# A transformer block with 32 experts on one Trainium2 core: the expert stage's bias, token weights and scatter rebuilt, a tenth weight slot, and a shorter front

## The chip, the cores and the metric

The kernel runs on one core of a Trainium2 chip, in one launch. What is measured is the device time of an execution in microseconds (us). Three runs of the kernel before took 1227.55, 1227.74 and 1229.18 us, so the median is 1227.74 us. One more execution was taken by the hardware profiler. It took 1228.12 us in all, and its trace spans 1226.4 us from the first instruction to the last.

The engines are called as in the profile: PE (TensorE, matmuls), PEld (its weight load), DVE (VectorE), ACT (ScalarE), POOL (GpSimd) and SP (SyncE, which here issues nearly all DMAs). PSUM is the memory that PE writes; SBUF is the large on-chip memory; HBM holds the inputs.

## The reference

One layer works on 256 tokens of width 1024, all in float32:

```
mod = silu(c) @ w_ada + b_ada                      # six rows of 1024
h   = rms_norm(x) * (1 + scale1) + shift1
z   = h @ w_in                                     # 1024 -> 7440
ys  = moba(z), gla(z), retention(z), sliding_window(z)   # four mixers of width 256
mixed = sum_n sigmoid(logits_n) * (ys_n @ w_branch[n])   # 1024 merge logits a branch, part of z
x   = x + gate1 * (mixed @ w_out)
h2  = rms_norm(x) * (1 + scale2) + shift2
weights = softmax(top4(h2 @ w_router + b_router))
for e in 32 experts:
    gu  = h2 @ w_gate_up[e] + b_gate_up[e]         # 1024 -> 2048
    act = min(glu,7) * sigmoid(1.702*min(glu,7)) * (clip(lin,-7,7) + 1)
    y  += combine[:, e] * (act @ w_down[e] + b_down[e])   # 1024 -> 1024
x   = x + gate2 * y
out = rms_norm(x) * g_final
```

Every token takes 4 of the 32 experts. All expert weights are read all the same: 8 MB of `w_gate_up` and 4 MB of `w_down` for each expert, 384 MB in all.

## The kernel before, in words

**The front** (to about 300 us). The six `mod` rows are made by DVE (`ada`: rows of `w_ada` times the activation, added up in `acs`; `ada_end` turns the 128 partial sums of a column into one by 8 transposes on PE and two DVE reductions). The input projection is done in blocks of 256 columns (`z_unit`). Each block of weights is split in two float32r parts, `wh` by ACT and `wl` by DVE (`split`, L340 and L341), and PE multiplies hi by hi, hi by lo and lo by hi (`z_part`, L354). The four mixers run as generators between these blocks. Then for each of the four branches the merge gates (`pz_m`), the up-projection (`pu`, L804) and the out projection (`pw`, L758) follow. `gate_rows` (L289) spreads a `mod` row over all partitions by 8 matmuls. The GLA gate (`pga`, L590) takes 24 matmuls, three for each of 8 chunks of channels. In the two softmax mixers each head's values are two matmuls into 64 partitions (L484, L485).

**Memory for weights.** Weights come into slots of 2 MB (128 partitions of 16 KB), or into halves of them in the front. A slot is a buffer of one of several pools: five in `ring`, three in `rx` (opened when the mixers' memory is given up), one in `r9` (opened when the front's memory is given up), nine in all. Another one, `sp`, is used once for `wg0_3`. `slot` hands them out in turn. A load waits on the SP queue until the last reader of its slot is done, and since SP issues in order, all loads behind it wait too. The order is written in the code:

```
units = [wg_src(0, j) for j in range(3)] + [wg_src(1, j) for j in range(4)]
units += [wd_src(0, j) for j in range(2)]
```

`wgE_J` is the J-th quarter of expert E's `w_gate_up`, `wdE_J` half of its `w_down`. The code reaches far ahead by itself: SP runs on as long as there is a free slot.

**The experts** go in quads (`b`, four experts) and pairs (`r`). An expert has 64 places (`CAP`) for its tokens. For a quad, `gather` makes one-hot matrices `pm` on DVE and multiplies the split activations `n2h`, `n2l` with them (`pg`, L998), which gives `he`. `gate_up_bias` (L1056) puts the bias into the two accumulators `ea` and `eb` by matmuls with a column of the identity, in float32. `gate_up_part` (L1065) adds the products, two column groups at a time. `swiglu` (L1038 to L1045) works on DVE and ACT, `act_t` (L1079) transposes its result, `down` (L1092) multiplies by `w_down`, and its result is multiplied by `gate2` on DVE (`oa`, `ob`). POOL multiplies the one-hots by the tokens' weights (`pc`, L1022), PE transposes these (`psm`, L1030), and `scatter` (L1102, float32) adds a pair's result to `x_sb`. The bias of `w_down` is added in four pieces between experts 8 and 15 (`pyb`, L968). `last_pair` treats experts 30 and 31 in pieces, so that the final norm can follow closely.

PE's order in all this is the program's order, with a few instructions placed by `issue_after`.

## Time and profile before

| | |
|---|---|
| median of three runs | 1227.74 us |
| profiled execution, in all | 1228.12 us |
| its span in the trace | 1226.4 us |
| PE busy | 1154.7 us, 94% |
| DVE, ACT, POOL busy | 452.1, 177.0 and 37.0 us |
| read from HBM | 467.81 MB, 382 GB/s over the span |
| the front, first to last instruction before the first expert matmul | 0 to 299.5 us |
| last weight bytes | about 1207 us |

Busy time of PE is not the same as PE being the limit: matmuls are pipelined and their ends are modelled. Read a stage by two questions: are the DMA engines saturated, and what do the engines wait for. An instruction's place in the code is its line, as L354.

### The profile page before, as it was taken

The page shows a single profiled execution, that of the slowest core. Times are in us where ns is not written, and L with a number is a line of the kernel's source. Part 1 is how long each engine was busy: PE and PEld are TensorE (multiplying, and loading weights), DVE is VectorE, ACT ScalarE, POOL GpSimd, SP SyncE. Part 2 cuts the span into 40 slices and gives each one's busy share as a digit, 9 for nine tenths or more (in the row PEclk, how much of TensorE's full clock was granted, in tenths as well). Part 3 has the DMA queues.
Part 4 walks back from the last instruction along what each step waited for, and adds up shares of the span by engine and source line. Part 5 has one row for each costly group of instructions (what it writes and reads, how often), then busy time and mean ns, then how long its engine had stood idle before and what let it go on. Part 6 is the DMA issues. An engine that isn't in the chain of part 4 may idle for free.

```text
span 1226.4 us, 14472 instructions
## 1 busy us (share of the span) xinstructions
PE 1154.7 (94%) x6204; PEld 563.6 (46%) x6204; DVE 452.1 (37%) x764; ACT 177.0 (14%) x293; POOL 37.0 (3%) x105
## 2 busy tenths in 40 slices
PE   6999999999999999999999999999989998999885
PEld 4788899996334333333333333333323332332234
DVE  4577698656222212223132232222221312131213
ACT  3456244444100000000000010000000000000001
POOL 2000000001010000000000000000000000000000
PEclk9999999999999999999999999999999999999998
DMA  9966569848899999999999999999999999999994
GB/s 329 340 267 222 191 236 395 344 187 335 362 429 428 428 428 427 425 428 429 428 428 428 426 428 428 427 427 426 430 428 428 428 428 428 427 428 428 428 421 150
DMA packets 63655, 469.85 MB, mean 383 GB/s; under 512 B 6361, under 2 KB 18754, under 8 KB 39266
## 3 DMA queue, kind: packets, MB, share of 16 engines
q1 hardware_dynamic: 62770, 467.38, 92.4%
q10 hardware_dynamic: 816, 1.49, 0.3%
q8 instruction: 50, 0.82, 0.3%
q14 instruction: 19, 0.16, 0.0%
HBM read 467.81 MB, written 1.05 MB: 382 GB/s over the span
## 4 chain that ended last, share of the span: by engine, by line
PE 70%; DMA 19%; DVE 7%; ACT 1%; issue 1%; POOL 0%; ACTq 0%; SPq 0%; POOLq 0%; DVEq 0%
PE ed L1092 14%; PE ea L1065 13%; PE eb L1065 13%; DMA wd<-in_w_down_dram 12%; DMA wg<-in_w_gate_up_dram 6%; PE pz_m L354 6%; PE py L1102 4%; PE pw L758 2%; PE pg L998 2%; PE pu L804 2%; PE eat L1079 1%; DVE el L1043 1%; DVE el L1045 1%; DVE es L1044 1%; PE psm L1030 1%
## 5 line engine op out<-in xcount | busy, mean ns | idle before, releaser
L1065 PE MATMUL ea<-wg,he 128*64 128x512 f32 x1024 | 279.9, 600 | 6.0 <-DMA wg<-in_w_gate_up_dram 5.6
L1065 PE MATMUL eb<-wg,he 128*64 128x512 f32 x1024 | 278.0, 594 | 0.0
L1092 PE MATMUL ed<-wd,aT 128*64 128x512 f32 x960 | 211.5, 595 | 7.9 <-DMA wd<-in_w_down_dram 6.7
L1039 DVE TENSOR_SCALAR eg<-ea 128x512 f32<-128x512 f32 x32 | 22.1, 692 | 352.5 <-PE ea L1065 349.1
L1065 PEld LDWEIGHTS eb<-wg,he 128*64 128x64 f32 x1024 | 78.4, 137 | 147.8 <-issue 147.7
L1041 ACT ACTIVATE es<-eg 128x512 f32<-128x512 f32 x32 | 20.2, 630 | 816.4 <-DVE eg L1039 816.4
L1065 PEld LDWEIGHTS ea<-wg,he 128*64 128x64 f32 x1024 | 72.1, 137 | 142.5 <-issue 122.9
L1092 PEld LDWEIGHTS ed<-wd,aT 128*64 128x64 f32 x960 | 67.4, 137 | 140.9 <-issue 127.1
L354 PE MATMUL pz_m<-hh,wh_m 128*128 128x256 f32 x256 | 73.1, 286 | 0.0
L354 PE MATMUL pz_m<-hh,wl_m 128*128 128x256 f32 x256 | 72.3, 282 | 0.9 <-DVE wl_m L341 0.9
L354 PE MATMUL pz_m<-hl,wh_m 128*128 128x256 f32 x256 | 71.8, 280 | 0.0
L1102 PE MATMUL py<-oa,sm 128*128 128x512 f32 x60 | 33.7, 643 | 19.5 <-DVE oa L1096 19.4
L1104 DVE TENSOR_TENSOR x_sb<-x_sb,py 128x512 f32<-128x512 f32 x60 | 41.2, 687 | 28.8 <-PE py L1102 28.7
L354 PEld LDWEIGHTS pz_m<-hh,wl_m 128*128 128x128 f32 x256 | 48.2, 188 | 1.3 <-DVE wl_m L341 1.3
L354 PEld LDWEIGHTS pz_m<-hh,wh_m 128*128 128x128 f32 x256 | 48.4, 189 | 0.7 <-ACT wh_b L340 0.3
L354 PEld LDWEIGHTS pz_m<-hl,wh_m 128*128 128x128 f32 x256 | 48.3, 189 | 0.1
L1095 DVE TENSOR_TENSOR oa<-ed,late 64x512 f32<-64x512 f32 x15 | 10.2, 683 | 94.6 <-PE ed L1092 94.6
L1022 POOL TENSOR_TENSOR pc<-pm,comb 128x128 f32<-128x128 f32 x64 | 23.9, 411 | 675.0 <-PE psm L1030 664.4
L1095 DVE TENSOR_TENSOR ob<-ed,late 64x512 f32<-64x512 f32 x15 | 10.2, 683 | 90.0 <-PE ed L1092 90.0
L1056 PE MATMUL ea<-bgu,ident 32*64 32x512 f32 x128 | 36.5, 612 | 0.0
L1056 PE MATMUL eb<-bgu,ident 32*64 32x512 f32 x128 | 36.5, 612 | 0.0
L1079 PEld LDWEIGHTS eat<-ident,el 128*128 128x128 f32 x128 | 17.8, 207 | 37.8 <-DVE el L1045 35.6
(443 smaller groups left out, 1398.4 us busy)
## 6 DMA issues: line engine op xcount, KB each, us to landing
wg<-in_w_gate_up_dram SPq DMA_DIRECT2D x128, 2048.0 KB, 27.7
wd<-in_w_down_dram SPq DMA_DIRECT2D x62, 2048.0 KB, 26.9
wada<-in_w_ada_dram SPq DMA_DIRECT2D x13, 1024.0 KB, 10.7
win_m<-in_w_in_dram SPq DMA_DIRECT2D x11, 1024.0 KB
win_c<-in_w_in_dram SPq DMA_DIRECT2D x8, 1024.0 KB, 16.5
wada<-in_w_ada_dram SPq DMA_DIRECT2D x12, 512.0 KB, 7.2
wada<-in_w_in_dram SPq DMA_DIRECT2D x4, 1024.0 KB, 7.5
win_m<-in_w_ada_dram SPq DMA_DIRECT2D x3, 1024.0 KB
```

What stands on the lines that cost most here:

```text
L354: T.matmul(pz[:, b * 256:(b + 1) * 256], l, r, start=(kh == 0 and b == 0 and kk == 0 and i == 0), stop=last and i == 2, skip_group_check=True)
L758: T.matmul(pw[t, hf_], m_[:, kk, t * P:(t + 1) * P], w[:, 0, :], start=(k == 0 and i == 0), stop=(k == KC - 1 and i == 2))
L804: T.matmul(pu[:, b * S:(b + 1) * S], w[:, k, b * P:(b + 1) * P], yx[:, k, :], start=(i == 0), stop=(i == 5), skip_group_check=True)
L998: last_i["pg"] = T.matmul(pg[:, kk * 256:(kk + 1) * 256], chan(n2[:, t, :], k), pm[:, t].rearrange("p e s -> p (e s)"), start=(i == 0), st ...
L1022: G.tensor_tensor(pc[:, t, :, var, i ^ var, :], pv_[:, :, i, :], cv[:, :, i].unsqueeze(2).to_broadcast([P, EB // 2, CAP]), ALU.mult)
L1039: V.tensor_scalar(g, pa, 7.0, None, ALU.min)
L1056: T.matmul(pp_[64 * j:64 * j + 64, :], ident[r:r + NE, r + e:r + e + 1].to_broadcast([NE, CAP]), bgu[r:r + NE, :], start=True, stop=False, ...
L1065: T.matmul(pp_[64 * j:64 * j + 64, :], he[:, k, (e % EB) * CAP:(e % EB + 1) * CAP], w[:, i * DE + j * 512:i * DE + (j + 1) * 512], start=F ...
L1079: T.transpose(pt[:, q * P:(q + 1) * P], cols, ident)
L1092: T.matmul(pd[64 * jj:64 * jj + 64, :], aT[:, k % 4, 64 * (k // 4):64 * (k // 4) + 64], w[k % 4][:, o * 512:(o + 1) * 512], start=(k == 0) ...
L1102: T.matmul(py, s_[:, hf_, t * P:(t + 1) * P], o, start=True, stop=True)
L1104: V.tensor_tensor(yv, yv, py, ALU.add)
```

## The change

All of it is in one kernel program; the sizes of the experts' weights and the order of the experts are the same.

1. **Bias.** `b_gate_up` is loaded three times, in three blocks of 32 partitions. POOL makes three bf16 parts of it that add up to the float32 value (seven instructions of 2048 elements a partition). A matmul in bf16 with 96 rows of `sel` (three stacked identities) puts the sum into the accumulators. `b_down` lies in the other 32 partitions.
2. **Token weights.** `slot_weights` brings the weights to the experts' 64 places (8 small matmuls and 3 reductions a quad), and `swiglu` multiplies by them. The products `pc` on POOL go; `spread` transposes the one-hots themselves.
3. **Scatter.** The result of `down` is split in hi and lo (ACT copy, DVE subtraction); the scatter is 8 float32r matmuls and runs inside the next pair's `gate_up`. The sums stand in `y_sb`, and `gate2` and `x` come in once, in `x_most`, before the last pair. All of `down_bias` is done at expert 4.
4. **Slots.** `hh` and `hl`, the split activations of the front, lie in one 2 MB buffer of pool `hp`, which becomes a tenth slot when they are no longer read. The one-off `sp` goes. The load order becomes `wg0_0` to `wg0_3`, `wg1_0` to `wg1_3`, `wd0_0`, `wd0_1`. `n2h` and `n2l` live only for the first quad; later gathers split `x_sb` again, a quarter at a time (`n2_split`). In `x_most` the tenth slot is taken for `gate2`, `g_final` and the sums.
5. **Front.** `gate1` is made by two matmuls of a broadcast one with `acs` (which sums the partitions and spreads the sum) and a row of `b_ada` that is loaded to all partitions (512 KB, on ACT's queue), in place of 8 transposes, 2 reductions, `gate_rows(2)` and 2 copies. The GLA gate's hi and lo columns are packed, 16 matmuls in place of 24. Values of the softmax mixers are multiplied for two heads at a time, in two column groups.

The core of the diff:

```diff
+        if s_ == 2:                                    # in ada_end
+                T.matmul(pb, ones[:, 0:1].to_broadcast([P, P]), acc[:, cs], start=True, stop=True)
+                V.tensor_tensor(gate1[:, cs], pb, gate1[:, cs], ALU.add)
...
-            for w, hx in ((wgah, hh), (wgah, hl), (wgal, hh)):
-                T.matmul(pg[0:16, 0:S], w[:, k, :], hx[:, k, :], start=(n == 0), stop=(n == 3 * KC - 1))
+            T.matmul(pg[0:32, 0:S], wgc[:, k, :], hh[:, k, :], start=(k == 0), stop=(k == KC - 1))
+            T.matmul(pg[0:16, 0:S], wgah[:, k, :], hl[:, k, :], start=False, stop=(k == KC - 1), skip_group_check=True)
...
-            if i > 0:
-                values(order[i - 1])
+            if i in (2, 4):
+                values(order[i - 2], order[i - 1])
...
+    A.dma_start(gate1, b_ada[0:1, 2 * D:3 * D].to_broadcast([P, D]))
...
+            for g in range(3):
+                A.dma_start(bt[NE * g:NE * g + NE, :], b_gate_up[0])
+            A.dma_start(bdn, b_down[0])
+            G.tensor_copy(bgu[0:3 * NE, :], bt[0:3 * NE, :])
+            for g0 in (1, 2):
+                for g in range(g0, 3):
+                    r = slice(NE * g, NE * g + NE)
+                    G.tensor_tensor(bt[r, :], bt[r, :], bgu[r, :], ALU.subtract)
+                    G.tensor_copy(bgu[r, :], bt[r, :])
...
+    units = [wg_src(e, j) for e in range(2) for j in range(4)] + [wd_src(0, j) for j in range(2)]
     for u in units[:RING + EXTRA]:
         pref[u[0]] = load_wide(*u)
+    add_slots(hp, 1)
+    for u in units[RING + EXTRA:-1]:
+        pref[u[0]] = load_wide(*u)
...
+        V.scalar_tensor_tensor(sg, sg, w, g, ALU.mult, ALU.mult)          # in swiglu, w: the places' weights
...
+        for jj in range(2):                                               # at the end of down
+            r = slice(64 * jj, 64 * jj + 64)
+            oh, ol = o[jj ^ sw]
+            A.activation(oh[r], pd[r], AF.Copy)
+            V.tensor_tensor(ol[r], pd[r], f32(oh[r]), ALU.subtract)
...
+                gate_up(e, he, range(2))                                  # a pair's start
+                with tc.issue_after(last_i["gu"]):
+                    scatter(*after)
+                gate_up(e, he, range(2, KC))
...
+    def x_most():
+        late = hp.tile([P, 4096], F32, tag="w", name="late")
+        seq.remove(hp)
+        A.dma_start(gfin[0:1, :], g_final.rearrange("(o d) -> o d", o=1))
+        V.tensor_tensor(y_sb, y_sb, gate2.unsqueeze(1).to_broadcast([P, NT, D]), ALU.mult)
+        V.tensor_tensor(xf, x_sb, y_sb, ALU.add)
```

On SP's queue, the loads of the first experts before the change, from the first on (the number at a name's end is that of its buffer):

```order
L134 DMA wg0_0_3154<-in_w_gate_up_dram 128x4096
L134 DMA wg0_1_3156<-in_w_gate_up_dram 128x4096
L134 DMA wg0_2_3158<-in_w_gate_up_dram 128x4096
L134 DMA wg1_0_3160<-in_w_gate_up_dram 128x4096
L134 DMA wg1_1_3162<-in_w_gate_up_dram 128x4096
L134 DMA wg1_2_3164<-in_w_gate_up_dram 128x4096
L134 DMA wg1_3_3166<-in_w_gate_up_dram 128x4096
L134 DMA wd0_0_3168<-in_w_down_dram 128x4096
L134 DMA wg0_3_3310<-in_w_gate_up_dram 128x4096
L134 DMA wd0_1_3312<-in_w_down_dram 128x4096
L134 DMA wd1_0_3522<-in_w_down_dram 128x4096
```

And after it, at the same place of SP's queue:

```order
L134 DMA wg0_0_3133<-in_w_gate_up_dram 128x4096
L134 DMA wg0_1_3135<-in_w_gate_up_dram 128x4096
L134 DMA wg0_2_3137<-in_w_gate_up_dram 128x4096
L134 DMA wg0_3_3139<-in_w_gate_up_dram 128x4096
L134 DMA wg1_0_3141<-in_w_gate_up_dram 128x4096
L134 DMA wg1_1_3143<-in_w_gate_up_dram 128x4096
L134 DMA wg1_2_3145<-in_w_gate_up_dram 128x4096
L134 DMA wg1_3_3147<-in_w_gate_up_dram 128x4096
L134 DMA wd0_0_3149<-in_w_down_dram 128x4096
L134 DMA wd0_1_3242<-in_w_down_dram 128x4096
L134 DMA wd1_0_3524<-in_w_down_dram 128x4096
```

`wg0_3` has moved up from ninth to fourth place and now sits in a slot that is used again. In both, ten loads stand ahead of `wd1_0`, the first that needs a slot which an expert's matmuls have to give back.

On PE, before the change, around the first expert's first quarters (`pg0_2` and `pg0_3` are the gather's third and fourth part; of the gather's matmuls before these rows 22 have run):

```order
L998 MATMUL pg0_2_3369<-pm0_3320,n2h_3138 128x256
L998 MATMUL pg0_2_3369<-pm0_3320,n2l_3251 128x256
L1065 MATMUL ea0_3314<-wg0_0_3154,he0_3330 64x512 x2
L1065 MATMUL eb0_3315<-wg0_0_3154,he0_3330 64x512 x2
L1065 MATMUL ea0_3314<-wg0_0_3154,he0_3330 64x512 x2
L1065 MATMUL eb0_3315<-wg0_0_3154,he0_3330 64x512 x2
L1065 MATMUL ea0_3314<-wg0_1_3156,he0_3330 64x512 x2
```

After it, at the same place:

```order
L1019 MATMUL pg0_3_3372<-pm0_3302,n2h_3250 128x256
L1019 MATMUL pg0_3_3372<-pm0_3302,n2l_3251 128x256
L1124 MATMUL ea0_3296<-wg0_0_3133,he0_3307 64x512 x2
L1124 MATMUL eb0_3297<-wg0_0_3133,he0_3307 64x512 x2
L1124 MATMUL ea0_3296<-wg0_0_3133,he0_3307 64x512 x2
L1124 MATMUL eb0_3297<-wg0_0_3133,he0_3307 64x512 x2
L1124 MATMUL ea0_3296<-wg0_1_3135,he0_3307 64x512 x2
```

30 of the first gather's 32 matmuls now stand ahead of the first expert's, where 24 stood.

On POOL, before the change, from the second mixer's norm to the first pair (`hrsret` is a small power, `ssq2` the router's norm, `pc0` the first quad's weighted one-hots):

```order
L518 TENSOR_TENSOR hrsret_1715<-hvarret_1712,mhalf_86 128x8
L902 TENSOR_TENSOR ssq2_3142<-ssq2_3142,mhalf_86 128x1 x2
L1022 TENSOR_TENSOR pc0_3605<-pm0_3320,comb_3298 128x2x64 x8
```

After it, at the same place:

```order
L528 TENSOR_TENSOR hrsret_1697<-hvarret_1694,mhalf_86 128x8
L794 CAST bias_sb_2303<-bgu32_2305 96x2048
L798 TENSOR_TENSOR bgu32_2305<-bgu32_2305,bias_sb_2303 32x2048 x2
L799 CAST bias_sb_2303<-bgu32_2305 32x2048 x2
L798 TENSOR_TENSOR bgu32_2305<-bgu32_2305,bias_sb_2303 32x2048
L799 CAST bias_sb_2303<-bgu32_2305 32x2048
L935 TENSOR_TENSOR ssq2_3120<-ssq2_3120,mhalf_86 128x1 x2
L1010 CAST pm0_3302<-pm0_3302 128x2x64 x2
```

Seven long instructions for the bias now stand between the mixers and the router; of the one-hots POOL copies two blocks a quad in place of eight products.

## Rows read from the trace of the kernel before

**Rows 1.** Stretches of the span: busy time of each engine, clock, DMA share, GB/s.
```profile
core 0: us, PE busy (x) PEld busy (x) DVE busy (x) ACT busy (x) POOL busy (x), PEclk, DMA share, GB/s
...
30.00:60.00 30.00, 28.46 (x240) 23.59 (x239) 16.87 (x37) 12.13 (x18) 0.00 (x0) 1.00 1.00 340
60.00:150.00 90.00, 89.26 (x673) 76.42 (x673) 67.53 (x132) 44.70 (x91) 2.56 (x1) 1.00 0.61 226
...
300.00:305.00 5.00, 5.00 (x26) 1.70 (x24) 2.54 (x10) 2.03 (x4) 1.78 (x5) 1.00 0.82 279
305.00:310.00 5.00, 5.00 (x28) 2.23 (x26) 0.54 (x1) 0.56 (x1) 1.13 (x4) 1.00 0.90 370
...
315.00:320.00 5.00, 5.00 (x27) 1.37 (x24) 2.67 (x4) 0.63 (x1) 0.00 (x0) 1.00 0.92 392
320.00:325.00 5.00, 5.00 (x24) 1.80 (x23) 0.69 (x1) 0.00 (x0) 0.00 (x0) 1.00 0.34 75
...
330.00:1195.00 865.00, 819.91 (x3690) 286.38 (x3688) 220.24 (x341) 35.34 (x59) 21.04 (x56) 1.00 1.01 427
1195.00:1207.00 12.00, 10.91 (x92) 7.01 (x89) 3.16 (x8) 0.00 (x0) 0.00 (x0) 1.00 0.86 305
1207.00:1227.00 20.00, 7.43 (x84) 6.00 (x82) 8.80 (x21) 3.08 (x8) 1.08 (x1) 0.81 0.17 61
```

**Rows 2.** What SP's queue waited for: us in total, times, longest us.
```profile
SPq L134 <- PE eb L1065: 406.9, 106, 13.5
```

**Rows 3.** Timeline of SP's queue: start us, us, the load issued.
```profile
303.19 0.33 SPq L134 DMA_DIRECT2D wd<-in_w_down_dram  x1
...
306.62 0.33 SPq L134 DMA_DIRECT2D wd<-in_w_down_dram  x1
...
311.36 0.33 SPq L134 DMA_DIRECT2D wg<-in_w_gate_up_dram  x1
...
322.64 0.33 SPq L134 DMA_DIRECT2D wg<-in_w_gate_up_dram  x1
```

**Rows 4.** What PE waited for from 60 to 300: us, times, longest.
```profile
PE pz_m L354 <- DVE wl_m L341: 0.9, 2, 0.7
```

**Rows 5.** The chain that ended last, in order: start us, us, instructions.
```profile
103.28 2.78 PE pga L590 x24
...
391.83 13.88 PE ed L1092 x64
...
408.57 3.82 PE py L1102 x8
```

**Rows 6.** Groups of PE, 60 to 300: count, busy us, mean ns, idle before.
```profile
L260 PE MATMUL pmt<-ident,acs 128*128 128x128 f32 x32 | 5.1, 286 | 0.0
...
L289 PE MATMUL pb<-ident,modT 128*128 128x128 f32 x32 | 4.1, 277 | 0.0
...
L484 PE MATMUL po<-pT,svt 128*64 128x256 f32 x8 | 2.6, 405 | 0.0
...
L485 PE MATMUL po<-pT,svt 128*64 128x128 f32 x8 | 1.6, 279 | 0.0
```

**Rows 7.** One stretch of the front, columns as in rows 1.
```profile
180.00:205.00 25.00, 25.00 (x212) 24.90 (x212) 21.50 (x28) 11.02 (x15) 0.00 (x0) 1.00 1.04 394
```

**Rows 8.** Groups of DVE in that stretch, 180 to 205.
```profile
L245 DVE SCALAR_TENSOR_TENSOR acs<-wada,cact,acs 128x1024 f32<-128x1024 f32 x6 | 7.7, 1276 | 0.0
L341 DVE TENSOR_TENSOR wl_m<-win_m,wh_m 128x1024 fp32r<-128x1024 f32 x6 | 7.3, 1222 | 3.5 <-ACT wh_m L340 3.5
```

**Rows 9.** Timeline of DVE around 365.5: start us, us.
```profile
365.64 0.68 DVE L1045 SCALAR_TENSOR_TENSOR el<-el,es 128x512 f32<-128x512 f32 x1
```

**Rows 10.** POOL's products from 360 to 370: duration in ns, min/median/max.
```profile
L1022 POOL TENSOR_TENSOR pc<-pm,comb x8: 397/398/880, 364.8 to 368.0; 128x128 f32<-128x128 f32 x8
```

**Rows 11.** Timeline of POOL around 365.5.
```profile
365.35 1.24 POOL L1022 TENSOR_TENSOR pc<-pm,comb 128x128 f32<-128x128 f32 x2
```

**Rows 12.** Groups of POOL, 0 to 140.
```profile
L172 POOL MEMSET tri<- 128x128 f32 x1 | 0.2, 206 | 0.0
...
L154 POOL MEMSET ones<- 128x64 f32 x1 | 0.2, 153 | 0.0
```

More of the change, by code (lines that the diff above doesn't have):

```diff
@@ L1036, in swiglu, with down_bias @@
-    def swiglu(pa, pb, e, name):
+    last_i = {}
+    def down_bias():
+        pct = bank("z", "pct")
+        for t in range(NT):
+            T.matmul(pct[3 * NE:, t * P:(t + 1) * P], comb[:, t, :], ident, start=True, stop=True)
+        cT = ep.tile([P, 512], F32, tag="eg", name="cT")[3 * NE:, 0:S]
+        V.tensor_copy(cT, pct[3 * NE:, 0:S])
+        for t in range(NT):
+            for hf_ in range(2):
+                cs = slice(hf_ * 512, hf_ * 512 + 512)
+                py = bank("t", f"pyb{t}{hf_}")
+                T.matmul(py, cT[:, t * P:(t + 1) * P], bdn[:, cs], start=True, stop=True, tile_position=(3 * NE, 0))
+                V.tensor_tensor(y_sb[:, t, cs], y_sb[:, t, cs], py, ALU.add)
@@ new lines, in gather_first @@
+    def gather_first(then):
+        pm, he = one_hot(0)
+        with tc.issue_after(last_i["pm"]):
+            n2_low(1, slice(0, 256))
+        for q in range(1, 4):
+            with tc.issue_after(last_i["pm"]):
+                for t in range(NT):
+                    n2_low(t, slice(q * 256, (q + 1) * 256))
+        for k2 in range(KC // 2):
+            cs = slice(k2 * 256, (k2 + 1) * 256)
+            gather_part(0, k2, pm, he, n2h[:, :, cs], n2l[:, :, cs])
+            then(k2, he)
+        return he, pm
@@ new lines, in n2_split @@
+    def n2_split(k2, name, after=()):
+        cs = slice(k2 * 256, (k2 + 1) * 256)
+        nh, nl = [epa.tile([P, NT, 256], F32R, tag=tg, name=f"{tg}{name}_{k2}") for tg in ("nh", "nl")]
+        with ExitStack() as st:
+            for i in after:
+                st.enter_context(tc.issue_after(i))
+            for t in range(NT):
+                A.activation(nh[:, t, :], x_sb[:, t, cs], AF.Copy, scale=rss[t])
+                V.scalar_tensor_tensor(nl[:, t, :], x_sb[:, t, cs], rss[t], f32(nh[:, t, :]), ALU.mult,
+                                       ALU.subtract)
+        return nh, nl
@@ L1098, in scatter @@
-    def scatter(e, s_, oa, ob):
+                last_i["ed"] = T.matmul(pd[64 * jj:64 * jj + 64, :],
+                                        aT[:, k % 4, 64 * (k // 4):64 * (k // 4) + 64],
+                                        w[k % 4][:, (jj ^ sw) * 512:(jj ^ sw) * 512 + 512], start=(k == 0),
+                                        stop=(k == KC - 1)).ins
+            if k % 4 == 3:
+                between[k // 4]()
+        for jj in range(2):
[3 more added lines that the diff above has]
+            V.tensor_tensor(ol[r], pd[r], f32(oh[r]), ALU.subtract)
@@ L1099, in scatter @@
+    def scatter(e, s_, o):
         for t in range(NT):
-            for hf_, o in enumerate((oa, ob)):
+            for hf_ in range(2):
                 py = bank("t", f"py{e}_{t}{hf_}")
-                T.matmul(py, s_[:, hf_, t * P:(t + 1) * P], o, start=True, stop=True)
-                yv = x_sb[:, t, hf_ * 512:(hf_ + 1) * 512]
-                V.tensor_tensor(yv, yv, py, ALU.add)
+                for i, o_ in enumerate(o[hf_]):
+                    T.matmul(py, s_[:, hf_, t * P:(t + 1) * P], o_, start=(i == 0), stop=(i == 1))
+                yv = y_sb[:, t, hf_ * 512:(hf_ + 1) * 512]
+                if e == 0:
+                    V.tensor_copy(yv, py)
+                else:
+                    V.tensor_tensor(yv, yv, py, ALU.add)
@@ L1309, in hybrid_block_kernel @@
+    he, pm = gather_first(first)
+    first_n2.close()
+    g0_i = last_i["pg"], last_i["pg"]
+    with tc.issue_after(last_i["he"]):
+        combine()
+    wsl = slot_weights(0, pm)
     ep = ctx.enter_context(tc.tile_pool(name="ep", bufs=1, side="right"))
-    g0_i = last_i["pg"], last_i["pg"]
-    late_sc = []
+    y_sb = ep.tile([P, NT, D], F32, tag="y", name="y_sb")
+    flag_i = None
+    after = None
+    nxt = None
     for b in range(NE // EB):
-        he, pm = he_n, pm_n
-        sm = None
@@ new lines, in hybrid_block_kernel, with second @@
+            gate_up(e + 1, he, range(2, KC))
+            act = swiglu(*gu.pop(e + 1), wsl[:, (e + 1) % EB:(e + 1) % EB + 1], f"{e + 1}")
+            more = iter(())
+            if r == 1:
+                more = gather_steps(b + 1)
+                nxt = next(more)
+            o = [[ep.tile([P, 512], F32R, tag=f"o{h}{i}", name=f"o{h}{i}{e}") for i in "hl"] for h in "ab"]
+            aT2 = []
+            def second():
+                with tc.issue_after(last_i["ed"]):
+                    aT2.append(act_t(e + 1, act))
+                next(more, None)
@@ L1344, in hybrid_block_kernel @@
+            down(e, aT, o, (second, lambda: next(more, None)))
+            down(e + 1, aT2[0], o, (lambda: next(more, None),) * 2)
+            if r == 1:
+                he, pm, wsl = nxt
+            if e == 0:
+                flag_i = overflow_flag()
+            after = e, sm, o
+            if e == 4:
+                down_bias()
     rs3 = cp.tile([P, 2 * NT], F32, tag="rs3", name="rs3")
```

351 lines of the change are left out of this document (169 added, 182 removed).

## The prediction

> **What bounds the kernel now.** I read the stretches of the span first [rows 1], because the question for each stage is whether the DMA engines or PE set its pace. From 330 to 1195 the DMA share is 1.01 at 427 GB/s; in all of that time loads go at a rate that never changes, while PE is busy 819.91 of 865 us. So the expert stage lasts as long as its weights take to come in, and PE follows them. What SP's queue waits for says the same from the other side: its long wait is for slots that PE gives back [rows 2], but the loads ahead of the waiting one keep the engines full. From 60 to 150 it is the other way: share 0.61, PE busy 89.26 of 90. What PE waits for in the front is almost nothing, 0.9 us for DVE's split [rows 4]. So the front goes at PE's pace and the experts at DMA's. Between the two lies a seam: 279 GB/s from 300 to 305, 370 to 310, 392 from 315 to 320 and only 75 from 320 to 325 [rows 1]. SP's timeline names the cause. The loads that need a slot back from expert 0 are issued at 303.19, 306.62 and 311.36, and the fourth only at 322.64 [rows 3]: the fourth quarter of expert 0 sits in a buffer that is used once and gives no slot back. At the end, weights flow until about 1207 and 20 us of last work follow, with clock 0.81 [rows 1].
>
> Two things can therefore shorten the time: PE work taken out of the front, which brings everything after it forward, and bytes moved in the seam. PE work taken out between 330 and 1195 brings nothing.
>
> **The front.** GLA gate: 24 matmuls take 2.78 us [rows 5], 0.116 each; 8 go: 0.9 us. gate1: eight of the 32 transposes that are busy 5.1 us go, at most 0.16 each, 1.3 us; so do 16 of the 32 PE instructions of L289 that are busy 4.1, 2.0 us [rows 6]. Two float32 matmuls of 512 columns come; the scatter's row has four such in 3.82 us over eight instructions [rows 5], so 1.9 us. Net 1.4, or 1.1 with the transposes at the spacing of L289 (0.13 us); I take 1.2. Attention values: eight heads have 16 instructions of 256 columns and 16 of 128, half of them in [rows 6]. An instruction of 512 columns alone costs 0.48 us (3.82/8), and in two column groups 13.88/64 = 0.22 [rows 5]. Alone they cost 16 x 0.24 + 16 x 0.12 = 5.7 us, in pairs 2.6; a gain of at most 3.1, and none if a pair waits for its second head's probabilities. I take 2.0. Sum of PE: 0.9 + 1.2 + 2.0 = 4.1 us, between 2 and 5.4.
>
> DVE loses two reductions and two copies and gains two additions of the same size; PE does not wait for it, so I put this at zero, covered by DVE's own idle time (67.53 busy of 90). Against the gain stands the row of b_ada, 512 KB, that ACT's queue loads near the start. There PE is busy only 28.46 of 30 us and DMA has share 1.00 at 340 GB/s [rows 1]: at 340 to 427 GB/s it costs 1.2 to 1.5 us, all of it on the path, or nothing if it falls where PE is ahead. I take 1.3. Net of the front: -2.8 us, between +1 and -5.4. The bias loads move 640 KB more than before, near 180, where [rows 7] has DMA share 1.04 and PE busy all of the time; PE covers them. If the cover fails they cost 1.6 us at 394 GB/s.
>
> **The seam.** In the new load order wg0_3 has a slot like the others, and ten loads still stand ahead of the first that needs a slot back. The releases come from PE. Six more of the gather's matmuls stand ahead of wg0_0's (0.116 each), so the first comes 0.7 us later; later ones not, since those six no longer stand between them. The slot of wg0_3 is released about 3.5 us after wg0_2's (the spacing of the first two, 303.19 and 306.62) and some 1 us of bias later, near 316, when the load ahead of it (three of 4.9 us each from 303.9, at 427 GB/s) has until 318.6 to run. Nothing is idle then until 323.5, and wg1_0's slot is free near 321. So the idle time goes: 5 x (1 - 75/427) = 4.1 us from 320 to 325 and 5 x (1 - 392/427) = 0.4 before it [rows 1]. Less the 0.7: -3.8 us. Bounds: -0 if the weights' products `pwt` hold PE up until the combine is ready, and -7.0 if the idle parts from 300 to 310 (1.7 and 0.7 us) go as well. The tenth slot alone brings no more, because ten loads were placed before the first release in both.
>
> **The experts.** Each pair loses PE work (bias in one pass of bf16, scatter in float32r) and gains an ACT copy and a DVE subtraction for each half, a split of a quarter of `x_sb` for each step of a gather. All of this lies beside loads at 427 GB/s, with PE idle some 45 us of 865 and ACT busy 35; I put it at zero. It costs something only if a release comes more than ten loads late, about 49 us, which no single wait here comes near; the longest at the slots is 13.5 us [rows 2]. The tail: `x_most` stands before the last pair, while weights still come in, and adds a 4 KB load that PE waits for and two DVE operations of 2048 elements. The work behind the last bytes is the same. I put it at zero, 0 to +3 if PE has not made up for the wait when the last weights land.
>
> **POOL's bias work.** The trace before has no POOL instruction of this size. From below: a POOL write of 128 elements takes 206 ns and of 64 takes 153 [rows 12], so 2048 elements take about 1.7 us; from above: a product of 128 elements takes 397 ns [rows 10], and 16 of them 6.4. Seven instructions: 12 to 45 us; I take 3 us each, 21 in all, nearer to the writes, because the products' start is a large part of them. Nothing waits for the result until 300. So by itself it costs nothing. What it might do to DVE is the rival below.
>
> The sum against the profiled execution is 1228.1 - 2.8 - 3.8 = 1221.5 us. The median of the runs is 0.4 lower than that execution, so I predict 1221 us.
>
> **Rival 1: POOL holds up DVE, slower.** At 365.64 DVE runs `el`, which reads two tensors in SBUF [rows 9]. Two products of POOL there take 1.24 us [rows 11] where two take 0.8 by the median, and the longest has 880 ns against 397 [rows 10]. So POOL stands still while such a DVE instruction runs. The reverse is not shown: `el` has its 0.68 us. If it holds, the bias work of 21 us, placed about 180 to 205, takes its time from a DVE that is busy 21.50 of 25 us there [rows 7], mostly with `wl_m` and `acs`, which have two inputs in SBUF [rows 8]. DVE would lose 21 less the 3.5 us idle, 17.5; PE has about 3 us of split weights ahead of it; so PE would be 14 us late, for good, since it is at its limit from there on. That gives 1221 + 14 = 1235. The point from which it decides is about 13 us of POOL time: from there the loss passes the 6.6 us of the sum. For it: the 880 ns. Against it: the row shows POOL as the one that waits, and `el` starts with a product still under way. Chance 0.23.
>
> The Trainium skill, page "SBUF — State Buffer", section "Who interferes with whom", says that a VectorE instruction with two SBUF inputs and a GpSimd instruction that reads SBUF lock each other out, and whoever starts first keeps the ports for its whole length. The 880 ns agree with one half of that; by the other half the time would come out at this rival's 1235. The page "GPSIMD Engine Reference", section 3.1, gives 4497 ns for an addition of 2048 float32 elements; as an estimate from this page, the three subtractions alone would be 13.5 us, and the rival's price would rise by a few us.
>
> **Rival 2: the seam moves and the front gives nothing, no change.** If a part of the front goes at DVE's pace (21.50 of 25 us busy) and the early 512 KB cost all of 1.5, PE's 4.1 us shrink to nothing, and with the combine before expert 1 half the idle time of the seam stays: 1228 - 2 = 1226. For it: DVE is nearly full where the merge runs. Against it: 0.9 us of waits in the whole front. Chance 0.15.
>
> **Rival 3: more than forecast.** PE's front gain of 4.1 without the early loss, and all idle time from 300 to 325 gone: 1227.7 - 4.1 - 7 = 1216.6. For it: in this reading the loads of the pairs never stop after the first. Against it: the first release cannot come before the first expert's matmuls. Chance 0.1.
>
> **How the numbers follow.** The forecast has 0.52: 1217 to 1225 by its own bounds. The range of 8 in 10 goes from 1215 to 1233: it leaves out the half of rival 1 with long POOL instructions, and holds the rest. A measurement of this kernel can tell 0.2%, 2.5 us, from no change. Faster by more (below 1225.3): forecast and rival 3, 0.6 with what the forecast's upper end gives to "same"; within: 0.15; slower (above 1230.2): rival 1 and a little of the tail's clock, 0.25.
>
> **What would show it.** Right: in the changed profile the stretch 315 to 325 (shifted by some 3 us) moves 420 GB/s or more; the first expert matmul starts at 296 to 298 instead of 299.5; from there to the last weights the rate is 427; the last 20 us are as before. Rival 1: `wl_m` or `acs` longer than 1.22 and 1.28 us, or gaps of DVE between them, beside the POOL casts, and PE waiting for `wl_m` by more than 0.9 us. Rival 2: the first expert matmul at 299 or later. The prediction is wrong in its base if the rate between 330 and 1195 is not 427, or if the work behind the last bytes grows.

## The result, and the profile after

The changed kernel takes 1238.82 us (median of four runs, 1236.36 to 1240.67), beside 1228.46 for the kernel before in the same series: 1.0083 times as long, interval 1.0063 to 1.0104. The forecast was 1221 us, faster. What came is rival 1, which had a chance of 0.23 and a price of 1235: the kernel is slower, because POOL's bias work holds up DVE and DVE holds up PE. The time lies above the range too (1215 to 1233), and 3.8 us above the rival's price.

First the same stretches of the changed kernel's trace, with the columns of [rows 1]:

```profile
180.00:205.00 25.00, 17.89 (x132) 17.08 (x130) 24.96 (x12) 7.59 (x10) 20.62 (x6) 0.93 1.04 380
300.00:305.00 5.00, 4.32 (x35) 3.92 (x34) 2.94 (x11) 2.35 (x7) 0.65 (x2) 1.00 1.01 431
305.00:310.00 5.00, 5.00 (x25) 5.00 (x26) 2.11 (x8) 3.03 (x8) 0.37 (x1) 0.51 1.00 423
310.00:315.00 5.00, 5.00 (x35) 3.97 (x35) 4.47 (x12) 0.27 (x1) 0.76 (x2) 0.81 0.43 179
315.00:320.00 5.00, 5.00 (x26) 1.89 (x27) 0.71 (x2) 1.48 (x3) 0.00 (x0) 1.00 0.01 2
320.00:325.00 5.00, 5.00 (x26) 1.70 (x24) 0.00 (x0) 0.00 (x0) 0.00 (x0) 1.00 1.00 360
330.00:1195.00 865.00, 803.84 (x3651) 299.74 (x3649) 252.23 (x430) 95.79 (x176) 4.17 (x14) 0.98 1.01 428
1217.00:1238.00 21.00, 8.57 (x88) 6.92 (x88) 9.25 (x22) 3.08 (x8) 1.17 (x1) 0.81 0.19 68
```

The first line answers to [rows 7]. There PE was busy all of 25 us with 212 instructions; now 17.89 us with 132. DVE's share looks better than before, 24.96 us busy, and that is the trap of the column: it did 12 instructions in place of 28. POOL, which was empty, is busy 20.62 us. So in this one stretch PE falls behind by 80 of its instructions. The granted clock (PEclk) is 0.93 where it was 1.00. The experts' line (428 GB/s) and the last one are as they were.

Now POOL and DVE side by side in this stretch, in order of time (start us, us, instruction; a row can join several):

```profile
184.03 1.97 POOL L794 CAST bias_sb<-bgu 96x2048 bf16<-96x2048 f32 x1 [28.52 <-DMA bgu<-in_b_gate_up_dram]
186.07 9.46 POOL L798 TENSOR_TENSOR bgu<-bgu,bias_sb 32x2048 f32<-32x2048 f32 x2
195.59 5.07 POOL L799 CAST bias_sb<-bgu 32x2048 bf16<-32x2048 f32 x2
200.74 4.38 POOL L798 TENSOR_TENSOR bgu<-bgu,bias_sb 32x2048 f32<-32x2048 f32 x1
205.19 2.77 POOL L799 CAST bias_sb<-bgu 32x2048 bf16<-32x2048 f32 x1
```

And DVE's rows, in the same columns:

```profile
184.16 2.38 DVE L348 TENSOR_TENSOR wl_b<-wada,wh_b 128x512 fp32r<-128x512 f32 x1
186.46 10.15 DVE L348 TENSOR_TENSOR wl_m<-win_m,wh_m 128x1024 fp32r<-128x1024 f32 x2
196.53 0.68 DVE L830 TENSOR_TENSOR msg<-pu,msg 128x512 f32<-128x512 f32 x1
197.14 1.77 DVE L348 TENSOR_TENSOR wl_b<-wada,wh_b 128x512 fp32r<-128x512 f32 x1
198.83 2.37 DVE L831 TENSOR_TENSOR mix<-mix,msg 128x512 f32<-128x512 f32 x1
201.13 7.91 DVE L348 TENSOR_TENSOR wl_m<-win_m,wh_m 128x1024 fp32r<-128x1024 f32 x2
```

Two `wl_m` take 10.15 us where one takes 1.22 [rows 8], and the two POOL subtractions beside them take 9.46. The engines alternate: a DVE instruction that starts beside a POOL instruction stands until that one ends, and then does its own work. `msg` keeps its 0.68 us in the midst of it; one of its two inputs, `pu`, is in PSUM. `mix`, of the same size with both inputs in SBUF, takes 2.37. What PE waits for from 60 to 300 (us, times, longest), where 0.9 us stood [rows 4]:

```profile
PE pz_m L361 <- DVE wl_m L348: 10.7, 5, 4.6
```

Of these 10.7 us, 2.9 stand before POOL's first instruction, and `e1_hi_only` below has the same 2.9. POOL's share is the other three waits, 7.8 us, and one of 1.6 us for `msg`.

Setting each PE instruction against the same one before gives the course of the loss (times of the kernel before, each trace from its own first instruction). The changed kernel is 1.9 us late at 30, 2.1 early at 147, 0.5 early at 188, 12.9 late at 203 and still 12.8 late at 290. So 13.4 us are lost between 188 and 203. Waits for DVE are 9.4 of them. The other 4.0 PE spends at a lower clock behind these waits: in the changed kernel's own time the granted clock is 0.61 from 191.6 to 196 and 0.50 to 0.57 from 206.2 to 213.5, and a `pz_m` matmul of 128x256 lasts 0.41 us there, 0.28 elsewhere.

From 290 on a second, smaller loss follows. The chain shows it (start us, us, instructions):

```profile
306.85 3.57 PE pb L296 x16
...
315.46 1.01 PE ea L1124 x4
```

PE's timeline before has the same 16 matmuls of `gate_rows` off the chain, which went by DVE there:

```profile
293.09 2.03 PE L289 MATMUL pb<-ident,modT 128*128 128x128 f32 x16
```

In the changed kernel PE was idle 0.7 us between 300 and 305; from 305 to 310 the granted clock is 0.51, nearly all at the lower of its levels (1.2 of 2.4 GHz), and 0.81 after that. So the first expert starts at 315.46, 16.0 us later than at 299.49. The span ends only 11.2 us later (1237.6 and 1226.4): 4.8 us come back behind the first expert. That is the seam.

Of the seam the rows show something that the forecast had otherwise. SP's timeline has the first loads that need a slot back at

```profile
319.08 3.76 SPq L134 DMA_DIRECT2D wd<-in_w_down_dram  x2
```

and the tenth load has landed by 314.5, so that the hole (179 and 2 GB/s, above) now lies ahead of the first release. The idle time did not go, it moved; what the tenth slot brings is that some 2 MB more have landed. Worked out from the rates of the traces, 93.0 MB have been read 25 us after the start of the first expert before the change, and 95.5 after it.

### The profile page after: what moved, and what is told of

It reads as the page before. It is cut to its first block, busy times and chain, and to the rows that moved or that the text cites. A ratio compares the mean times of both kernels' runs of the same rounds, so it can differ in the third digit from the quotient of the medians.

```text
span 1237.6 us, 14530 instructions
## 1 busy us (share of the span) xinstructions
PE 1137.6 (92%) x6134; PEld 580.3 (47%) x6134; DVE 499.1 (40%) x845; ACT 236.0 (19%) x409; POOL 41.6 (3%) x64
## 4 chain that ended last, share of the span: by engine, by line
PE 72%; DMA 16%; DVE 9%; issue 1%; ACT 1%; POOL 0%; POOLq 0%; ACTq 0%; DVEq 0%; SPq 0%
PE ea L1124 15%; PE ed L1150 14%; PE eb L1124 14%; DMA wg<-in_w_gate_up_dram 9%; PE pz_m L361 6%; DMA wd<-in_w_down_dram 6%; PE pg L1019 3%; PE pw L768 2%; PE py L1167 2%; DVE wl_m L348 1%; PE pu L823 1%; PE eat L1138 1%; DVE y_sb L1172 1%; DVE nl L1055 1%; DMA wada<-in_w_ada_dram 1%
## 5 line engine op out<-in xcount | busy, mean ns | idle before, releaser
L361 PE MATMUL pz_m<-hhl,wh_m 128*128 128x256 f32 x512 | 96.9, 289 | 0.6 <-ACT wh_m L347 0.6
L361 PE MATMUL pz_m<-hhl,wl_m 128*128 128x256 f32 x256 | 73.9, 289 | 10.7 <-DVE wl_m L348 10.7
L361 PEld LDWEIGHTS pz_m<-hhl,wh_m 128*128 128x128 f32 x512 | 81.4, 195 | 1.5 <-ACT wh_m L347 0.8
L361 PEld LDWEIGHTS pz_m<-hhl,wl_m 128*128 128x128 f32 x256 | 49.9, 195 | 11.7 <-DVE wl_m L348 11.7
L1172 DVE TENSOR_TENSOR y_sb<-y_sb,py 128x512 f32<-128x512 f32 x56 | 36.0, 684 | 37.8 <-PE py L1167 37.8
L1019 PE MATMUL pg<-pm,nl 128*128 128x256 f32 x112 | 36.7, 344 | 15.7 <-DVE nl L1055 15.4
L1019 PE MATMUL pg<-pm,nh 128*128 128x256 f32 x112 | 34.6, 316 | 17.1 <-ACT nh L1054 17.1
L348 DVE TENSOR_TENSOR wl_m<-win_m,wh_m 128x1024 fp32r<-128x1024 f32 x26 | 44.7, 1732 | 7.6 <-ACT wh_m L347 7.6
L1054 ACT ACTIVATE nh<-x_sb,ssq 128x256 fp32r<-128x256 f32 x56 | 25.3, 499 | 80.3 <-PE pg L1019 80.3
L347 ACT ACTIVATE wh_m<-win_m 128x1024 fp32r<-128x1024 f32 x26 | 27.5, 1059 | 66.1 <-PE pz_m L361 51.4
```

The source lines that it names most:

```text
L347: A.activation(wh, src, AF.Copy)
L348: V.tensor_tensor(wl, src, f32(wh), ALU.subtract)
L361: T.matmul(pz[:, b * 256:(b + 1) * 256], l, r, start=(kh == 0 and b == 0 and kk == 0 and i == 0), stop=last and i == 2, skip_group_check=True)
L1019: last_i["pg"] = T.matmul(pg[:, kk * 256:(kk + 1) * 256], n2[:, t, :].rearrange("p (c r) -> p r c", r=2)[:, kk, :], pm[:, t, :, 0:2], star ...
L1054: A.activation(nh[:, t, :], x_sb[:, t, cs], AF.Copy, scale=rss[t])
L1172: V.tensor_tensor(yv, yv, py, ALU.add)
```

## The experiments

All times are medians; the ratio is against the kernel before in the same series (medians 1228.46 to 1229.08 us), with its interval in brackets. A gain in us is a difference of medians. The first question is whether POOL's work alone is the loss, and whether by its reads or by its mere running.

**Without the two lower parts of the bias.** `e1_hi_only` keeps one POOL instruction of the seven; the output lacks the two lower parts.

```diff
-            for g0 in (1, 2):
-                for g in range(g0, 3):
-                    G.tensor_tensor(bt[r, :], bt[r, :], bgu[r, :], ALU.subtract)
-                    G.tensor_copy(bgu[r, :], bt[r, :])
+            V.memset(sel, 0.0)      # blocks 1 and 2 of sel stay zero
```

> The changed kernel with the two lower bf16 parts of the bias left out (its output has a coarser bias): POOL does one cast of 96x2048 in the front instead of seven instructions; loads, slots and matmuls stay as they are. Theory A (POOL instructions that read SBUF stop DVE instructions with two inputs in SBUF, 24 us of them): the 13.4 us that PE loses between 188 and 203 go, and with them some 1 to 2 us of low clock behind; 1238.8 - 13.4 - 1.5 = 1224 us (1222 to 1226). Rival B (the larger bias loads and their half slot are what makes the front late): 1236 to 1239, as the loads are unchanged. Rival C (most of the loss lies in the experts' rebuilt work): no lower than 1232.

Measured: 1226.11, ratio 0.9971 (0.9959 to 0.9982). Six instructions less bring 12.7 us; its stretch from 180 to 205 has 205 of the 212 PE instructions back:

```profile
180.00:205.00 25.00, 24.45 (x205) 24.14 (x204) 19.20 (x24) 9.72 (x13) 2.16 (x1) 1.00 1.03 378
```

What is left is 3.0 us faster than the kernel before, where the forecast had 6.6.

**The burst alone, in the kernel before.** `e2_before_burst` puts POOL instructions of the same kinds and about as many elements into the kernel before, on data that nothing waits for. They have half the elements each, are twice as many, and take 31.0 us of POOL in all, where the seven take 23.65.

```diff
+    G.tensor_copy(scr[0:3 * NE, 0:512], bgu[0:3 * NE, :])
+    G.tensor_copy(scr[0:3 * NE, :], x_sb[0:3 * NE, h, :])                   # 2 of these
+    G.tensor_tensor(scr[r, :], x_sb[r, h, :], scr[r, :], ALU.subtract)      # 6 of these
+    G.tensor_copy(scr[r, :], x_sb[r, h, :])                                 # 6 of these
```

> The kernel before, with POOL instructions added after the retention mixer's norm that read x and a scratch tile and write only the scratch (14 of 1024 elements and one of 512, as much work as the changed kernel's seven of 2048); nothing waits for them. Theory A: POOL is busy some 24 us between 155 and 185, DVE idles 3 to 4 us there before, PE has a small lead: 1228.5 + 8 to 13 = 1236 to 1242 us. Rivals B and C: POOL's work by itself costs nothing, 1228 to 1230.

Measured: 1239.87, ratio 1.0092 (1.0074 to 1.0109), 10.8 us. Its stretch from 180 to 205, columns as before, and then its groups (count, busy us, mean ns, idle before):

```profile
180.00:205.00 25.00, 20.39 (x157) 19.65 (x155) 25.00 (x16) 8.43 (x11) 22.96 (x12) 0.93 1.04 395
```

DVE's groups from 182 to 212:

```profile
L341 DVE TENSOR_TENSOR wl_m<-win_m,wh_m 128x1024 fp32r<-128x1024 f32 x5 | 11.8, 2372 | 0.0
...
L264 DVE TENSOR_TENSOR modT<-ade,bT 128x4 f32<-128x4 f32 x1 | 2.1, 2106 | 0.0
L823 DVE TENSOR_TENSOR msg<-pu,msg 128x512 f32<-128x512 f32 x3 | 2.0, 677 | 0.0
```

POOL's:

```profile
L788 POOL TENSOR_TENSOR scr<-x_sb,scr 32x1024 bf16<-32x1024 f32 x6 | 16.4, 2734 | 0.5
L790 POOL CAST scr<-x_sb 32x1024 bf16<-32x1024 f32 x6 | 10.0, 1672 | 0.4
```

Work whose result nobody needs costs as much as the whole regression (10.4 us). `modT` is the clearest row: an addition of 4 columns, 152 ns elsewhere, lasts 2106 ns and ends with the POOL subtraction beside it.

**Reads or writes.** `e3_writes` is the first experiment with 13 POOL memsets added, 24.0 us of POOL time, as much as the changed kernel's seven instructions.

```diff
+    for _ in range(13):
+        G.memset(bt[0:3 * NE, :], 0.0)
```

> As the kernel with the two lower bias parts left out, with 13 POOL writes (memset of 96x2048 float32) behind the one cast: POOL is as busy in the same place, some 22 us, but reads nothing. Theory A (it is reads of SBUF that lock): the same time as without them, within 1 us, near 1224. Rival D (any POOL work in that stretch holds DVE up, by writes too): 1234 to 1239.

Measured: 1225.78, ratio 0.9979 (0.9969 to 0.9989), the same as without them. The stretch:

```profile
180.00:205.00 25.00, 24.01 (x199) 23.50 (x199) 21.05 (x25) 10.04 (x14) 21.21 (x12) 1.00 1.04 382
```

DVE's groups from 180 to 206:

```profile
L245 DVE SCALAR_TENSOR_TENSOR acs<-wada,cact,acs 128x1024 f32<-128x1024 f32 x4 | 5.1, 1274 | 0.0
...
L243 DVE TENSOR_SCALAR acs<-wada,cact 128x1024 f32<-128x1024 f32 x1 | 1.5, 1499 | 0.0
```

POOL is busy 21.21 us, and `acs` with two SBUF inputs has its 1.27 us. So it is not a busy POOL that holds up DVE's instructions with two inputs in SBUF, but one that reads SBUF. `L243`, with one input, takes 1499 ns in place of 746 beside a memset: one instance that this does not cover.

**The bias as it was.** `e4_bias32` is the changed kernel with float32 bias as before: no POOL work, PE does the bias in float32 (`b_down` then lies in two halves).

```diff
-            G.tensor_copy(bgu[0:3 * NE, :], bt[0:3 * NE, :])      # and the six that follow
+            bgu = lb.tile([P, 512], F32, tag="bgu", name="bgu")   # 4 loads, as before the change
```

> The changed kernel with part 1 undone: the gate_up bias as in the kernel before (float32 matmuls with identity columns, 256 KB loaded, no POOL work), b_down in two halves of 512 columns; the rest as changed. Theory A: as without the lower parts, and 0.5 us later in the seam because a bias in float32 takes 1 us instead of 0.5 once ahead of expert 0: 1223 to 1226, faster than before by 2 to 5 us. If the bf16 bias had been worth something in the expert stage: 30 experts x 0.5 us = up to 15 us more, 1238 or above.

Measured: 1228.41, ratio 1.0001 (0.999 to 1.0013). It was to show what is left of the change, 1223 to 1226, and shows nothing gained. The profiled execution was the quickest of its runs (1224.54), so no trace shows what the others spent. This result is not explained.

**Splitting the bias without POOL.** `e5_split_wide` does the split on ACT and DVE in 128 x 512 (a quarter of the columns in each block of partitions) and moves the parts with 12 small loads on ACT's queue.

```diff
-            G.tensor_copy(bgu[0:3 * NE, :], bt[0:3 * NE, :])      # and the six that follow
+                    A.activation(part, src, AF.Copy)
+                    V.tensor_tensor(src, src, part, ALU.subtract)
+                    A.dma_start(bgu[NE * g:NE * g + NE, q * 512:(q + 1) * 512], part[NE * q:NE * q + NE, :])
```

> The changed kernel, complete, with the three bf16 parts made by ACT (three casts of 128x512) and DVE (two subtractions of 128x512) at the branch loop's last branch, and brought to their three blocks of partitions by 12 small loads from SBUF; POOL has no bias work. Theory A: DVE pays 2 x 0.68 us instead of being locked out for 24 us of POOL time; the 13.4 us go as in the run without the lower parts, and the one cast's lock (2.2 us) too: 1223 to 1226. If the 12 small loads get in the way of the weights: 1228 and above.

Measured: 1226.44, ratio 0.9978 (0.9969 to 0.9987), 0.4 above the expected range. The split stood at 180 on ACT, which waited 8.0 us for a bias load there, and PE lost 4.0 us between 147 and 190 (2.4 early to 1.6 late). POOL was free of it, and the place was still a bad one. It is 2.0 us faster than `e4_bias32`, which differs in the bias alone, although its trace has PE 4.2 us behind that kernel's at 285 (1.6 late, 2.6 early). So the float32 bias seems to cost time behind the front. From 900 to 1190 PE is busy 274.84 of 290 us with it and 260.40 here; that this is the cause is not shown.

**The early loads, behind the first work.** `e6_late` is that kernel with the gate's loads and the 512 KB row issued by ACT after a later copy.

```diff
-    A.dma_start(gate1, b_ada[0:1, 2 * D:3 * D].to_broadcast([P, D]))      # and the three before it
+    with tc.issue_after(zv_i["sq"].ins):
+            A.dma_start(wgg[16 * i:16 * i + 16], w_gla_gate[0])
...
+        A.dma_start(gate1, b_ada[0:1, 2 * D:3 * D].to_broadcast([P, D]))
```

> The same, with the four loads of the GLA gate's weights and of gate1's row issued by ACT behind the copy of z_sq (about 70 us) instead of ahead of csig. Theory E (what the early loads cost is ACT's time to issue four DMAs ahead of csig, 2.2 us on the way to the first projection): 2 us less than the kernel that differs only in this, 1221 to 1224. Rival (it is their 512 KB on a saturated DMA): the cost moves with them to where DMA is idle, so 1.2 us less at most.

Measured: 1226.81, ratio 0.998 (0.9972 to 0.9989). No gain, where 2 us were expected: what it won at the start (PE 0.4 us late at 30, `e5_split_wide` 1.8) it lost in the attention stage (1.4 us early at 147, `e5_split_wide` 2.4). `e8_bias32_late` is the same edit on the kernel with the float32 bias.

```diff
+    with tc.issue_after(zv_i["sq"].ins):      # around the same loads, in e4_bias32
```

> The kernel with the float32 bias, with the late front loads. Theory E: 2 us under the kernel with the float32 bias and early loads (1228.4), 1226.4. If the bias in bf16 is worth nothing in the experts, because they go at the pace of the weights: equal to the kernel with the split by ACT and DVE and late loads, within 1 us. If it is worth something there (PE's order or clock): 2 us and more above it.

Measured: 1228.43, ratio 0.9997 (0.9987 to 1.0007). No gain here either, and 1.6 us above `e6_late`, which differs from it in the bias alone.

**Without the tenth slot.** `e7_no_tenth` is `e6_late` with nine slots.

```diff
-    add_slots(hp, 1)
-        seq.remove(hp)
```

> As the kernel with the late front loads, but without the tenth slot (nine slots; wd0_1 waits for wg0_0's). Theory F (DMA-bound from the first release on, so one load fewer placed ahead of it is one load of 4.9 us later at the end): 1226 to 1229. Rival (the seam is paced by PE's releases, not by the number of slots): within 1 us of the kernel with the tenth slot.

Measured: 1230.95, ratio 1.0025 (1.0016 to 1.0035): 4.1 us slower than with it, and above the expected 1226 to 1229. With nine slots, all of them used again, 93.1 MB have been read 25 us after the first expert's start, as many as before the change (93.0). So the seam's gain is the slot's.

**The split later.** In `e9_split_late` it stands behind the third branch's last sigmoid (231 to 242), and the early loads go by SP's queue.

```diff
+    if at == 11:      # issued after the sigmoid of the third branch
-    A.dma_start(gate1, b_ada[0:1, 2 * D:3 * D].to_broadcast([P, D]))
+    nc.sync.dma_start(gate1, b_ada[0:1, 2 * D:3 * D].to_broadcast([P, D]))
```

> The changed kernel, complete: the bias split by ACT and DVE and brought to its place by small loads, now behind the sigmoid of the third branch's last block (about 225 us) instead of about 180, where ACT stood 8 us for the bias to land and issued 12 loads while the merge waited (4.4 us lost on PE between 174 and 190); the GLA gate's weights and gate1's row loaded from SP's queue in its own order. Theory G (what is missing against the forecast was lost there, by ACT, and by ACT's four early issues): the front's 4 us and the seam's 4 us both come through, 1220 to 1223, ratio 0.993 to 0.996. Rival (DMA or the experts' rebuilt work take it back): 1226, as in the runs with the split at 180.

Measured: 1224.76, ratio 0.997 (0.9959 to 0.9981), 1.8 us above the expected range. PE is 4.3 us early at 147, 2.8 from 179 on and 1.4 from 245 on. The first step stands before the split; the second follows it: the 12 small loads, 7.4 us of ACT's queue, make ACT late for the last branch. The clock falls once more ahead of `gate_rows` (0.66 from 290 to 295; 3.5 us for its 16 matmuls).

**The front alone.** `e11_front_only` is the kernel before with part 5 and nothing else.

```diff
+    T.matmul(pg[0:32, 0:S], wgc[:, k, :], hh[:, k, :], start=(k == 0), stop=(k == KC - 1))
+    A.dma_start(gate1, b_ada[0:1, 2 * D:3 * D].to_broadcast([P, D]))
+    values(order[i - 2], order[i - 1])
```

> The kernel before with part 5 of the change alone (gate1 by two matmuls and a loaded row, packed GLA gate, values for two heads at a time; the four loads issued by ACT early, as in the change). Forecast's term: PE work -4.1 us, early loads +1.3 to 2.2: 1226 (1225 to 1227), ratio 0.998. Rival (the front goes at DVE's pace in the merge): 1228 to 1229, the gain gone by 200 us.

Measured: 1227.01, ratio 0.9981 (0.9971 to 0.999): 2.3 us by the ratio and 1.7 by the medians, where the forecast had 2.8.

**Late split, small loads on SP.** `e12_split_sp` does all three casts first and issues the 12 small loads from SP's queue; the early loads go by SP's queue as in `e9_split_late`.

```diff
-    A.dma_start(bgu[NE * g:NE * g + NE, q * 512:(q + 1) * 512], part[NE * q:NE * q + NE, :])
+    nc.sync.dma_start(bgu[NE * g:NE * g + NE, q * 512:(q + 1) * 512], parts[g][NE * q:NE * q + NE, :])
```

> The changed kernel, complete, with the bias split by ACT and DVE behind the third branch's last sigmoid as in the run before, but the 12 small loads are issued at the end and from SP's queue, so that ACT issues nothing there. Theory G: in the run before, PE was 4.4 us early until 249 and 1.1 us early after it, because ACT (three casts, 12 issues, two waits for their landing between 231 and 242) came late with the split of out-projection and merge weights; most of those 3.2 us come back: 1221 to 1223.5, ratio 0.994 to 0.996. Rival: SP stands behind the small loads and wg0_1 to wg0_3 come late, or the 3 us are taken back in the seam: 1224 to 1226, as before.

Measured: 1221.14 (1219.91 to 1223.81), ratio 0.994 (0.9925 to 0.9955). It beats both kernels. Its stretches:

```profile
180.00:205.00 25.00, 25.00 (x212) 24.90 (x211) 20.97 (x27) 10.17 (x14) 0.00 (x0) 1.00 1.04 395
295.00:300.00 5.00, 5.00 (x35) 3.16 (x35) 2.95 (x8) 1.47 (x3) 0.00 (x0) 1.00 0.39 162
300.00:305.00 5.00, 5.00 (x26) 1.69 (x24) 0.00 (x0) 0.00 (x0) 0.00 (x0) 1.00 0.61 197
330.00:1190.00 860.00, 796.68 (x3645) 298.16 (x3642) 248.48 (x420) 93.81 (x174) 4.15 (x14) 0.99 1.01 427
```

The first line is [rows 7] again: 212 PE instructions, POOL empty. In its groups of DVE from 182 to 212 the split has its length back:

```profile
L348 DVE TENSOR_TENSOR wl_m<-win_m,wh_m 128x1024 fp32r<-128x1024 f32 x8 | 9.8, 1219 | 4.0 <-ACT wh_m L347 4.0
```

In its groups of PE from 284 to 305 so have the 16 matmuls of `gate_rows`:

```profile
L296 PE MATMUL pb<-ident,modT 128*128 128x128 f32 x16 | 2.0, 280 | 0.0
```

And in its chain the first expert starts 2.1 us before 299.49:

```profile
297.41 1.01 PE ea L1132 x4
```

**And without a `gate_rows` whose result is not used.**

```diff
-        gate_rows(5, "ab")
```

> The same without the 8 matmuls that spread the gate2 row before the first gather, whose result the changed kernel no longer reads. They took 3.5 us on PE at a granted clock of 0.66, between the router's last product and the second half of the positions. If they are on the way to the first gather: 1 to 2 us less than with them. Rival: PE waits there for DVE's choice of experts anyway, so nothing, or the clock is lower for longer: within 0.5 us, or up to 1 us more.

Measured: 1222.78, ratio 0.9956 (0.9941 to 0.997): not faster than with it, and by the medians 1.6 us slower, though the two intervals overlap. In both kernels the gather waits for ACT's `n2h` and starts at 293.5, so that the 2 us of PE turn into idle time. Behind this the clock falls: the granted clock is 0.59 from 290 to 295 and 0.72 from 295 to 300, where it is 1.00 with `gate_rows` in place. The chains show the 30 matmuls of the gather, here and then in `e12_split_sp`:

```profile
293.50 5.70 PE pg L1025 x30
```

```profile
293.57 3.84 PE pg L1027 x30
```

So the first expert starts at 299.21 in place of 297.41. In these two executions the matmuls whose result nobody reads kept PE at its full clock.

## Why the prediction was wrong, step by step

**The step that failed** is "Nothing waits for the result until 300. So by itself it costs nothing." POOL's time was priced well (21 us; the seven instructions measure 23.65, 1.97 + 9.46 + 5.07 + 4.38 + 2.77), but its cost was looked for where its result is used, and it lies in what its reads keep from DVE. The burst alone costs 10.8 us, taking six of seven away gives 12.7 back, and writes of the same length cost nothing. So the mechanism is shown from both sides, by runs of its own.

**Rival 1 had the price and not the chance.** It set 17.5 us of DVE time and 14 us of PE's; PE lost 13.4 between 188 and 203. The rows bear out the first: from 184.16 to 209.04 DVE does eight instructions that take 7.6 us by themselves, so it stands 17.3 us. The second meets its number in part by luck, since only 9.4 us are waits and 4.0 come from the lower clock behind them, a term that the rival did not have. The evidence against it was one place where POOL was seen waiting and DVE was not [rows 9, 11]. That place could not tell: `el` takes 0.68 us and a POOL product there 0.4, so a wait of DVE is at most as long as what is left of 0.4 us. Where POOL's instructions are ten times as long, so are the waits. The Trainium skill, page "SBUF — State Buffer", section "Who interferes with whom", has this rule in both directions, with an exception for GpSimd instructions that only write; the stretched `wl_m`, the unchanged `msg` and the memsets beside an unchanged `acs` agree with each part of it. One row that could not show the reverse direction was no ground for a chance of 0.23. The Trainium skill, page "GPSIMD Engine Reference", section 3.1, gives 4497 ns for an addition of 2048 float32 elements; the subtractions of that length here agree with 4.38 us, and 4.73 as the mean of two.

**Where the 17.8 us lie.** By the spans the kernel is 11.2 us slower, where the forecast had it 6.6 faster. The lead of the front at 147 is 2.1 in place of 2.8 (0.7). Of that lead 1.6 us are gone by 188, ahead of the long waits; `e11_front_only` and `e12_split_sp`, in which no bias work stands there, keep their leads, so this belongs to the bias part; which piece of it is not shown. Then come the 13.4, and 3.2 from 290 to the first expert, of which the forecast had 0.7. The seam gives 0.3 more than forecast. With rounding that makes 17.9.

**What came beside it.** The loss from 290 on was in no step. Part of it is the clock: `gate_rows` takes 3.57 us in place of 2.03, at 0.51, behind small idle times in the router stage. How much of these 1.5 us would come back at full clock is not tested; `e12_split_sp` has `gate_rows` at full clock, and `e13_no_dead` shows 30 other matmuls there 1.9 us longer at the lower one.

**The front** was right in size: PE gains 4.0 us from 30 (1.9 late) to 147 (2.1 early), and 4.1 in `e11_front_only`, forecast 4.1; part 5 alone is worth 1.7 to 2.3, forecast 2.8. The forecast's worst bound for it, +1 us, does not come out of its terms: 2 us less 1.5 is still a gain. The early loss was put at 1.3 us of bandwidth. The trace shows another way to it: four DMA issues on ACT's queue end at 7.64, where ACT's first work began at 6.16 before. ACT's timeline after:

```profile
6.09 0.79 ACTq L706 DMA_DIRECT2D wgg<-in_w_gla_gate_dram  x2
6.93 0.28 ACTq L707 DMA_DIRECT2D wgg<-in_b_gla_gate_dram  x1
7.25 0.36 ACTq L709 DMA_DIRECT2D gate<-in_b_ada_dram  x1
7.64 1.28 ACT L214 ACT_TABLE_LOAD   x1 [7.64 <-DMA wgg<-in_b_gla_gate_dram]
```

These 1.5 us are ACT's. How the 1.9 divide between issue and bandwidth is not settled: issuing them later on ACT made PE start 0.4 us late only, but the time did not fall, and the kernels that use SP's queue differ in more than that.

**The seam** was right in size and half right in reason: 4.8 us come back behind the first expert (16.0 late there, 11.2 at the end), forecast 4.5 (3.8 and the 0.7 of the gather), and the slot alone measures 4.1. But the text has "the tenth slot alone brings no more", and that sentence is wrong: without it the gain is gone (`e7_no_tenth`). In the changed kernel and in `e12_split_sp` the ten loads land before PE releases anything, and the hole stands there (162 and 197 GB/s from 295 to 305). More slots, not a steadier release, are what the seam pays for.

**The experts and the tail** came out at zero as forecast: 428 against 427 GB/s, and some 20 us of work behind the last bytes in both.

**The sum.** 1221 was the time of a kernel in which the bias split costs nothing, and `e12_split_sp`, where it nearly does, takes 1221.14. That the other terms add up to about what was forecast is likely from this kernel, but the nearness is partly luck: its interval is some 2 us to each side, and its early loads go by another queue. The float32-bias version at 1228.4 does not fit that sum, and stays open.

## What to carry to other kernels

An engine that is idle in the profile is not free to fill: ask what its instructions keep from the engine beside it, and price it by its whole length, since a neighbour that starts behind it waits for all that is left of it. In the table by stretches read the count of instructions beside the busy time; a DVE at 24.96 of 25 us that did 12 instructions in place of 28 is a DVE that stands still. An engine that waits can also pay twice, first the wait and then a lower clock. A split that nothing waits for still needs a place: on ACT at 180, on ACT's queue at 240 and on SP's queue at 240 the same work came to 1226.4, 1224.8 and 1221.1 us (the early loads too went from ACT's to SP's queue between the first and the second).
